# Smaller second load, one warm-up product for three, latents' transposes a chunk later in a one-core decoder layer

## The chip, the cores and the metric

One core of a Trainium2 chip runs the whole kernel. The metric is device time in microseconds. A row of a trace is stamped in microseconds from the start of the profiled span. TensorE is PE, VectorE is DVE, ScalarE is ACT, GpSimd is POOL, and SyncE (SP) issues the loads.

## The reference

For 256 tokens of width 1024 the layer computes, in float32:

```
proj = x @ W_in                      # c_q 256, c_kv 128, k_rope 32, then q, k, v of group B, 512 each
A = latent attention: rms_norm(c_q) @ w_uq, rms_norm(c_kv) @ w_ukv, rotary keys, 8 heads, causal
B = block attention over q, k, v of 8 heads; 256 keys are one block, so it is causal with ALiBi
x = LayerNorm(2**0.25 * x + concat(A, B) @ w_o)
x = LayerNorm(2**0.25 * x + FFN(x))  # FFN: up to 2*2816, causal conv of width 3, silu(g)*u, down
```

## The kernel before, in words

Every float32 operand of a large product is split in two rounded halves: `split` (lines 81 to 89) lets ACT cast the loaded tile to its high part `h_...` (L87) and DVE subtract to get the low part `l_...` (L88). A product is then three matmuls: high by high, high by low, low by high.

The stage that matters here is the first one. The input, transposed, comes in eight slices of 128 rows (`xraw`, 128 KB each), and so does the part of W_in that makes the latents (`w_c`: 128 rows by 416 columns, 208 KB a slice). `C_CHUNKS` says how many slices one load takes, as pairs (first slice, number); for each chunk SP issues the load of `xraw`, then that of `r_wc`, and each slice is cast and subtracted on its own. PE then accumulates `pc` for both halves of the tokens: six matmuls of 416 columns for a slice (L181 to L183). Before any data is there, `keep_warm` (L97 to L101) has PE multiply a zeroed tile: six products of 128 by 128, then three with 64 columns; in float32 each product is two matmul instructions.

Next come the values of group B, `pv` (L247): eight slices of w_v, six matmuls of 512 columns each. Inside this stage the normalised latents `cn` (they share the tile `ccn` with their transposed copy `cT`) are turned by PE, six 128 by 128 transposes into `pct` (L233); DVE scales each pair of them out of PSUM (L235), and ACT and DVE split the result into `chl` (L236, L237). `TURN_AFTER` is the slice of `pv` after which this is put. The queue projections `pq`, keys `pk` and the first `pqk` follow; then the heads' scores `sca`.

On PE the products of `pv`, the warm-up products and the transposes are pinned to the order in which they are written; from the first scores on, all matmuls are. What is not pinned is put in order by the framework's scheduler, which works from estimated costs: so a move of the transposes also moves instructions on DVE and ACT and the not yet pinned `pk`, `pq` and `pqk` products. Each engine then works its own list in order, and waits where an operand is not ready.

Of the kernel before, what the change touches and what calls it, by code (L numbers as in the profile page):

```python
# [14 lines left out]
P = 128  # L15
# [13 lines left out]
NEG = -1.0e30  # L29
CH = 1024  # L30

C_CHUNKS = ((0, 1), (1, 2), (3, 2), (5, 2), (7, 1))
V_CHUNKS = ((0, 2), (2, 2), (4, 2), (6, 2))
TURN_AFTER = 4
LAG = 2
BEFORE = 2
A0, A4 = 2, 0
WARM = (6, 5)
WARM_NARROW = 3
HELD = 6  # L40
HALVES = ((0, 512), (512, 512))
COLS = ((HALVES, HALVES), (HALVES, ((0, 512), (512, 256), (768, 256))))
# [9 lines left out]
def layer_kernel(ctx: ExitStack, tc: tile.TileContext, a, out):  # L52
    nc = tc.nc
# [11 lines left out]
    def wk_tile(name):  # L65
        return ps_wk.tile([P, HALF], F32, tag="wk", name=name)
# [27 lines left out]
    zero = const.tile([P, P], F32, name="zero")  # L94
    nc.vector.memset(zero, 0.0)

    def keep_warm(n, name, cols=P):  # L97

        warm = wk_tile(name)
        for _ in range(n):  # L100
            tc.keep_in_program_order(nc.tensor.matmul(warm[:, :cols], zero, zero[:, :cols], start=True, stop=True))  # L101

    keep_warm(WARM[0], "warm0")
    keep_warm(WARM_NARROW, "warm0n", P // 2)

    tabs = const.tile([P, 4], F32, name="tabs")

# [18 lines left out]
    wc = {}  # L126
    for k0, n in C_CHUNKS:
        ks = slice(k0, k0 + n)
# [98 lines left out]
    def turn_latents():  # L227
        for b0 in range(0, NB, 2):
            pt = wk_tile(f"pct{b0}")
            for b in range(b0, min(b0 + 2, NB)):  # L230
                for t in range(NT):
                    o = (b - b0) * S + t * P
                    tc.keep_in_program_order(nc.tensor.transpose(pt[:, o:o + P], cn[:, t, b * P:(b + 1) * P], ident))  # L233
                g = qg[:, b:b + 1] if b < 2 else kvg
                nc.vector.tensor_scalar(cT[:, b, :], pt[:, (b - b0) * S:(b - b0 + 1) * S], g, None, op0=ALU.mult)  # L235
        nc.scalar.copy(chi, cT)  # L236
        nc.vector.tensor_sub(clo, cT, chi.bitcast(F32))  # L237

    pv = [acc_tile(f"pv{t}") for t in range(NT)]
    for k0, n in V_CHUNKS:  # L240
        hi, lo = load_split(a["w_v"][:, k0 * HALF:(k0 + n) * HALF], n * HALF, f"wv{k0}", parts=n)
        for k in range(k0, k0 + n):
            o = (k - k0) * HALF
            for t in range(NT):
                tk = slice(t * P, (t + 1) * P)
                for i, (st, mv) in enumerate(((xhi, hi), (xhi, lo), (xlo, hi))):
                    tc.keep_in_program_order(nc.tensor.matmul(pv[t], st[:, k, tk], mv[:, o:o + HALF],  # L247
                                                              start=(k == 0 and i == 0), stop=(k == KT - 1 and i == 2)))
            if k == TURN_AFTER:
                turn_latents()  # L250
# [311 lines left out]

    a0, a4 = Turned(0, 0, 4, wk_tile), Turned(0, 4, 4, wk_tile)
    keep_warm(WARM[1], "warm1")
    a0.affine(True, 0, A0)
    ln_root(0, 1)
# [228 lines left out]
```

## Time and profile before

| what | value |
|---|---|
| median of 3 runs | 310.29 us (309.94 to 311.3) |
| the profiled execution | 308.82 us, of which the traced span is 307.0 us |
| PE busy | 296.1 us, 96% of the span |
| DVE, ACT, POOL busy | 77%, 65%, 10% |
| the chain that ended last | PE 92%, DVE 3%, DMA 2%, ACT 1% |
| mean granted TensorE clock | 0.994 |

The busy shares say that PE is the engine to look at; the chain of waits says the same by another way, since it follows the last instruction back to what released it. What is left is to find the few places where PE waits or runs slowly. The rows further down are from those places.

### The profile page before, as it was taken

To read this page: it belongs to the slowest core of one execution; us is meant where nothing else is said; L and a number is where in the kernel's file an instruction comes from. 1 tells how busy PE (TensorE), PEld (TensorE's weight loads), DVE (VectorE), ACT (ScalarE), POOL (GpSimd) and SP (SyncE) were. 2 spreads that over 40 slices of the span, in tenths; PEclk is the share of its full clock that TensorE was granted. 3 is DMA by queue.
4 is the path that set the end of the run, shared out by engine and by line. 5 is a ranking of instruction groups with operands and counts; after the bars stand their busy time and mean duration, and the time that the engine had idled before them with its cause. 6 is when DMAs were issued, how large, how long until landed. Compare 5 with 4: busy or idle time off the path is not lost.

```text
span 307.0 us, 4884 instructions
## 1 busy us (share of the span) xinstructions
PE 296.1 (96%) x1736; PEld 262.2 (85%) x1736; DVE 237.3 (77%) x475; ACT 198.8 (65%) x390; POOL 31.4 (10%) x43
## 2 busy tenths in 40 slices
PE   8999999999999989999999999999999999999990
PEld 7987999999888869888888888888888888888880
DVE  2878976656565387999999888888886978975595
ACT  4789996676655287977666657666676758634410
POOL 9430300035310021000000000000000000000030
PEclk9999999999999999999999999999999999999997
DMA  6998855273332104988865556555555776000003
GB/s 198 400 405 298 292 190 175 100 244 117 118 108 101 68 0 125 360 315 269 276 226 181 181 194 203 185 176 181 183 175 203 240 244 202 0 0 2 0 1 138
DMA packets 16216, 54.31 MB, mean 177 GB/s; under 512 B 1824, under 2 KB 2736, under 8 KB 16192
## 3 DMA queue, kind: packets, MB, share of 16 engines
q1 hardware_dynamic: 15840, 52.92, 49.7%
q0 software_dynamic: 352, 1.09, 1.2%
q8 instruction: 13, 0.21, 0.3%
q14 instruction: 11, 0.09, 0.1%
HBM read 52.95 MB, written 1.05 MB: 176 GB/s over the span
## 4 chain that ended last, share of the span: by engine, by line
PE 92%; DVE 3%; DMA 2%; ACT 1%; SPq 0%; issue 0%; DVEq 0%
PE ph L621 25%; PE pd L658 19%; PE ph L624 13%; PE pqk L279 7%; PE pm L279 7%; PE pv L247 4%; PE po L279 3%; PE pq L279 2%; PE sca L279 2%; DMA r_wc<-in_w_c 2%; PE scb L279 2%; PE pc L181 1%; PE ph L611 1%; PE ph L612 1%; PE ph L615 1%; PE pc L182 1%
## 5 line engine op out<-in xcount | busy, mean ns | idle before, releaser
L621 PE MATMUL ph<-x,h_wu 128*128 128x512 f32 x328 | 82.8, 393 | 0.0
L621 PEld LDWEIGHTS ph<-x,h_wu 128*128 128x128 f32 x328 | 59.1, 188 | 10.9
L88 DVE TENSOR_TENSOR l_wu<-r_wu,h_wu 128x1024 fp32r<-128x1024 f32 x44 | 53.5, 1219 | 7.7 <-ACT h_wu L87 7.3
L87 ACT CAST h_wu<-r_wu 128x1024 fp32r<-128x1024 f32 x44 | 45.8, 1048 | 6.2 <-PE ph L621 3.3
L633 DVE SCALAR_TENSOR_TENSOR hc<-h,cw,hc 128x255 f32<-128x255 f32 x82 | 39.3, 479 | 12.6 <-ACT hc L631 11.7
L624 PEld LDWEIGHTS ph<-x,l_wu 128*128 128x128 f32 x328 | 44.7, 190 | 3.4
L624 PE MATMUL ph<-x,l_wu 128*128 128x256 f32 x328 | 45.7, 282 | 0.0
L631 ACT ACTIVATE hc<-h,cw 128x256 f32<-128x256 f32 x41 | 24.6, 601 | 24.1 <-DVE h L628 24.1
L279 PE MATMUL pqk<-x,h_wqk 128*128 128x256 f32 x128 | 27.2, 298 | 0.0
L279 PEld LDWEIGHTS pqk<-x,h_wqk 128*128 128x128 f32 x128 | 20.6, 190 | 0.3
L88 DVE TENSOR_TENSOR l_wd<-r_wd,h_wd 128x1024 fp32r<-128x1024 f32 x16 | 19.5, 1220 | 0.9 <-ACT h_wd L87 0.9
L658 PE MATMUL pd<-l_wd,ghi 128*128 128x512 f32 (+1 forms) x80 | 20.1, 349 | 0.0
L658 PE MATMUL pd<-h_wd,glo 128*128 128x512 f32 (+1 forms) x80 | 20.1, 349 | 0.0
L658 PE MATMUL pd<-h_wd,ghi 128*128 128x512 f32 (+1 forms) x80 | 20.0, 348 | 0.0
L722 POOL TENSOR_TENSOR r<-r,lnv 128x512 f32<-128x512 f32 x1 | 1.3, 1293 | 180.8 <-ACT r L721 180.8
L279 PE MATMUL pqk<-x,l_wqk 128*128 128x256 f32 x64 | 19.1, 299 | 0.0
L628 DVE TENSOR_TENSOR h<-ph,hb 128x256 f32<-128x256 f32 x41 | 17.1, 417 | 2.0 <-ACT hb L626 2.0
L87 ACT CAST h_wd<-r_wd 128x1024 fp32r<-128x1024 f32 x16 | 16.7, 1045 | 2.8 <-PE ph L621 2.6
L645 ACT CAST ghi<-gt 128x256 fp32r<-128x256 f32 x22 | 8.9, 403 | 11.6 <-DVE gt L642 11.6
L658 PEld LDWEIGHTS pd<-h_wd,glo 128*128 128x128 f32 x80 | 14.0, 189 | 2.1
L658 PEld LDWEIGHTS pd<-l_wd,ghi 128*128 128x128 f32 x80 | 14.0, 189 | 2.1
L658 PEld LDWEIGHTS pd<-h_wd,ghi 128*128 128x128 f32 x80 | 14.0, 189 | 1.9
(166 smaller groups left out, 583.6 us busy)
## 6 DMA issues: line engine op xcount, KB each, us to landing
r_wu<-in_w_up SPq DMA_DIRECT2D x44, 512.0 KB, 3.7
r_wd<-in_w_down SPq DMA_DIRECT2D x22, 512.0 KB, 4.2
r_wqk<-in_w_qk SPq DMA_DIRECT2D x8, 512.0 KB, 5.1
r_wo<-in_w_o SPq DMA_DIRECT2D x8, 512.0 KB, 3.9
r_wv<-in_w_v SPq DMA_DIRECT2D x4, 512.0 KB, 7.7
lnv<-in_ln SPq DMA_DIRECT2D x4, 512.0 KB, 5.8
r_wc<-in_w_c SPq DMA_DIRECT2D x3, 416.0 KB, 6.6
r_wuq<-in_w_uq SPq DMA_DIRECT2D x2, 512.0 KB, 7.8
```

The costliest lines, as they stand in the source:

```text
L87: nc.scalar.copy(hi[:, c], raw[:, c])
L88: nc.vector.tensor_sub(lo[:, c], raw[:, c], hi[:, c].bitcast(F32))
L181: nc.tensor.matmul(pc[t][:, :NC0], xhi[:, k, tk], hi[:, o:o + NC0], start=(k == 0), stop=False)
L247: tc.keep_in_program_order(nc.tensor.matmul(pv[t], st[:, k, tk], mv[:, o:o + HALF], start=(k == 0 and i == 0), stop=(k == KT - 1 and i == 2)))
L279: ins = nc.tensor.matmul(*args, **kw)
L621: nc.tensor.matmul(ph, hi[:, ks], x1[:, k].rearrange("p i t -> p (i t)"), start=(k == 0), stop=False)
L624: nc.tensor.matmul(ph[:, :S], lo[:, ks], x1hi[:, k, :], start=False, stop=(k == KT - 1))
L628: nc.vector.tensor_tensor(h, ph[:, :S], hb, op=ALU.add)
L631: nc.scalar.activation(hc, h, AF.Identity, bias=c[:, 3:4], scale=c[:, 2:3])
L633: nc.vector.scalar_tensor_tensor(hc[:, j:S], h[:, 0:S - j], c[:, 2 - j:3 - j], hc[:, j:S], op0=ALU.mult, op1=ALU.add)
L645: rounded = nc.scalar.copy(ghi, gt)
L658: ins = nc.tensor.matmul(pd[t, o][:, :n], st[:, tk], mv[:, o:o + n], start=(f == 0 and i == 0), stop=(f == NF - 1 and i == 2))
```

## The change

Three numbers are changed. The first two slices are loaded one by one and the other six in pairs, where it was one, three pairs, and one. The warm-up is seven products of 128 columns and none of 64. The latents' transposes stand after slice 5 of `pv`, not after slice 4.

```diff
-C_CHUNKS = ((0, 1), (1, 2), (3, 2), (5, 2), (7, 1))
+C_CHUNKS = ((0, 1), (1, 1), (2, 2), (4, 2), (6, 2))
-TURN_AFTER = 4
+TURN_AFTER = 5
-WARM = (6, 5)
-WARM_NARROW = 3
+WARM = (7, 5)
...
-    def keep_warm(n, name, cols=P):
+    def keep_warm(n, name):
...
-            tc.keep_in_program_order(nc.tensor.matmul(warm[:, :cols], zero, zero[:, :cols], start=True, stop=True))
+            tc.keep_in_program_order(nc.tensor.matmul(warm[:, :P], zero, zero, start=True, stop=True))
 
     keep_warm(WARM[0], "warm0")
-    keep_warm(WARM_NARROW, "warm0n", P // 2)
```

Line numbers of the changed kernel are one or two lower than those used here. The numbers behind the tiles' names tell buffers apart; they differ between the two kernels where the tile is the same.

On ACT, at the start, the casts stood like this (the first `r_wc` is slice 0):

```order
L87 CAST x_101<-xraw 128x256
L87 CAST h_wc_105<-r_wc_103 128x416
L87 CAST x_101<-xraw 128x256 x2
L87 CAST h_wc_114<-r_wc_112 128x416 x2
L87 CAST x_101<-xraw 128x256 x2
```

and now stand like this:

```order
L86 CAST x_98<-xraw 128x256
L86 CAST h_wc_102<-r_wc_100 128x416
L86 CAST x_98<-xraw 128x256
L86 CAST h_wc_111<-r_wc_109 128x416
L86 CAST x_98<-xraw 128x256 x2
L86 CAST h_wc_120<-r_wc_118 128x416 x2
```

Slice 1 is now cast when it has come alone, and slices 2 and 3 come together. DVE's subtractions are moved in the same way.

On DVE, from the last scaling of the latents by their root to the first `qT`, in before (`l_wqk_436` is the low part of the first group-B weights, `chl` the low part of the turned latents):

```order
L235 TENSOR_SCALAR ccn_240<-pct0_333,vecs_181 128x256
L88 TENSOR_TENSOR l_wuq0_381<-r_wuq0_378,h_wuq0_380 128x1024
L235 TENSOR_SCALAR ccn_240<-pct0_333,vecs_181 128x256
L235 TENSOR_SCALAR ccn_240<-pct2_340,vecs_181 128x256
L88 TENSOR_TENSOR l_wuq1_387<-r_wuq1_384,h_wuq1_386 128x1024
L88 TENSOR_TENSOR l_wukv_393<-r_wukv_390,h_wukv_392 128x1024
L237 TENSOR_TENSOR chl_276<-ccn_240,chl_276 128x768
L88 TENSOR_TENSOR l_wqk00_436<-r_wqk00_433,h_wqk00_435 128x1024
L88 TENSOR_TENSOR l_wqk10_576<-r_wqk10_573,h_wqk10_575 128x1024
L312 TENSOR_TENSOR qT_376<-pq0_419,qtab_186 128x512
```

and now:

```order
L87 TENSOR_TENSOR l_wuq0_378<-r_wuq0_375,h_wuq0_377 128x1024
L233 TENSOR_SCALAR ccn_237<-pct0_336,vecs_178 128x256
L87 TENSOR_TENSOR l_wuq1_384<-r_wuq1_381,h_wuq1_383 128x1024
L233 TENSOR_SCALAR ccn_237<-pct0_336,vecs_178 128x256
L233 TENSOR_SCALAR ccn_237<-pct2_343,vecs_178 128x256
L87 TENSOR_TENSOR l_wukv_390<-r_wukv_387,h_wukv_389 128x1024
L87 TENSOR_TENSOR l_wqk00_433<-r_wqk00_430,h_wqk00_432 128x1024
L235 TENSOR_TENSOR chl_273<-ccn_237,chl_273 128x768
L87 TENSOR_TENSOR l_wqk10_573<-r_wqk10_570,h_wqk10_572 128x1024
L87 TENSOR_TENSOR l_wqk01_632<-r_wqk01_629,h_wqk01_631 128x1024
L310 TENSOR_TENSOR qT_373<-pq0_416,qtab_183 128x512
```

A weight subtraction now stands ahead of the first scaling, and another ahead of `chl`'s low part and of `qT`.

On PE, behind `pv` and the transposes of the rotary keys, ten products of the first `pqk` have moved ahead of those of `pk` and `pq` that need the low part of `chl`; it now reads:

```order
L277 MATMUL pq_416<-chl,h_wuq_377 128x256
L277 MATMUL pq_416<-chl,l_wuq_378 128x256
L277 MATMUL pqk_436<-x_98,h_wqk_432 128x256 x2
L277 MATMUL pqk_436<-x_98,l_wqk_433 128x256
L277 MATMUL pqk_436<-x_98,h_wqk_432 128x256 x2
L277 MATMUL pqk_436<-x_98,l_wqk_433 128x256
L277 MATMUL pqk_436<-x_98,h_wqk_432 128x256 x2
L277 MATMUL pqk_436<-x_98,l_wqk_433 128x256
L277 MATMUL pqk_436<-x_98,h_wqk_432 128x256
L277 MATMUL pk_407<-chl,h_wukv 128x256 x2
```

In before, `pk` and `pq` went on after the second of these rows, and all 24 products of `pqk` came behind them.

## Rows read from the trace of the kernel before

**Rows 1.** Page, chain that ended last: shares of the span by engine.

```profile
PE 92%; DVE 3%; DMA 2%; ACT 1%; SPq 0%; issue 0%; DVEq 0%
```

**Rows 2.** Timeline, PE, 0 to 17 us: start, us, engine, line, out<-in, count, [idle before].

```profile
1.05 2.93 PE L101 MATMUL warm<-zero 128*128 128x128 f32 x12 [1.05 <-DVE zero L95]
...
3.77 1.38 PE L101 MATMUL warm0n<-zero 128*128 128x64 f32 x6
...
5.47 1.06 PE L181 MATMUL pc<-h_wc,x 128*128 128x416 f32 x2 [0.32 <-ACT h_wc L87]
...
6.33 0.55 PE L182 MATMUL pc<-l_wc,x 128*128 128x416 f32 x1
...
7.37 0.55 PE L183 MATMUL pc<-h_wc,x 128*128 128x416 f32 x1
...
7.96 1.06 PE L181 MATMUL pc<-h_wc,x 128*128 128x416 f32 x2
...
8.82 0.55 PE L182 MATMUL pc<-l_wc,x 128*128 128x416 f32 x1
...
9.52 0.36 PE L182 MATMUL pc<-l_wc,x 128*128 128x416 f32 x1
...
16.48 0.35 PE L183 MATMUL pc<-h_wc,x 128*128 128x416 f32 x1
```

**Rows 3.** Windows: stretch, length, busy us of each engine, granted clock, DMA share, GB/s.

```profile
5.40:9.40 4.00, 3.88 (x10) 3.02 (x11) 2.78 (x6) 2.42 (x7) 3.80 (x4) 1.00 0.96 350
```

**Rows 4.** Timeline, ACT and DVE, the splits of slices 0 to 4.

```profile
4.88 0.54 ACT L87 CAST h_wc<-r_wc 128x416 fp32r<-128x416 f32 x1 [1.18 <-DMA r_wc<-in_w_c]
...
5.57 0.71 ACT L87 CAST x<-xraw 128x256 fp32r<-128x256 f32 x2 [0.15 <-DMA xraw<-in_xT]
...
7.37 0.98 ACT L87 CAST h_wc<-r_wc 128x416 fp32r<-128x416 f32 x2 [1.08 <-DMA r_wc<-in_w_c]
7.94 1.40 DVE L88 TENSOR_TENSOR l_wc<-r_wc,h_wc 128x416 fp32r<-128x416 f32 x2 [1.17 <-ACT h_wc L87]
...
9.69 0.98 ACT L87 CAST h_wc<-r_wc 128x416 fp32r<-128x416 f32 x2 [0.55 <-DMA r_wc<-in_w_c]
```

**Rows 5.** Timeline, PE, DVE and ACT, around the transposes.

```profile
23.11 1.98 ACT L87 CAST h_wuq<-r_wuq 128x1024 fp32r<-128x1024 f32 x2
...
23.51 0.38 PE L233 MATMUL pct<-ident,ccn 128*128 128x128 f32 x2
23.93 0.48 DVE L235 TENSOR_SCALAR ccn<-pct,vecs 128x256 f32<-128x256 f32 x1 [0.97 <-PE pct L233]
24.34 1.21 DVE L88 TENSOR_TENSOR l_wuq<-r_wuq,h_wuq 128x1024 fp32r<-128x1024 f32 x1
...
24.47 0.66 PE L233 MATMUL pct<-ident,ccn 128*128 128x128 f32 x4 [0.58 <-DVE ccn L235]
...
25.47 0.87 DVE L235 TENSOR_SCALAR ccn<-pct,vecs 128x256 f32<-128x256 f32 x2
```

**Rows 6.** Chain in order of time: start, us, what; `pv` behind the transposes.

```profile
25.13 4.10 PE pv L247 x18
```

**Rows 7.** Timeline, ACT, DVE and PE, from the turned latents to the first scores.

```profile
26.25 1.21 DVE L88 TENSOR_TENSOR l_wuq<-r_wuq,h_wuq 128x1024 fp32r<-128x1024 f32 x1
...
27.39 1.22 DVE L88 TENSOR_TENSOR l_wukv<-r_wukv,h_wukv 128x1024 fp32r<-128x1024 f32 x1
...
28.52 0.95 DVE L237 TENSOR_TENSOR chl<-ccn,chl 128x768 fp32r<-128x768 f32 x1
28.59 0.59 ACT L252 COPY v_b<-pv 128x512 f32<-128x512 f32 x1 [0.43 <-PE pv L247]
...
29.21 0.37 PE L279 MATMUL pk<-chl,h_wukv 128*128 128x256 f32 x1
...
29.39 2.35 DVE L88 TENSOR_TENSOR l_wqk<-r_wqk,h_wqk 128x1024 fp32r<-128x1024 f32 x2
...
31.66 0.68 DVE L312 TENSOR_TENSOR qT<-pq,qtab 128x512 f32<-128x512 f32 x1
...
34.29 0.82 PE L279 MATMUL sca<-kT,qT 128*128 128x128 f32 x4
```

## The prediction, made before the changed kernel ran

> **What bounds the kernel now.** I read the chain of waits first: 92% of it is PE [rows 1], so a change counts by what it does to PE's list, and whatever PE loses or wins in the first 35 us is carried to the end, unless a later wait takes it up. Then the timeline of PE in the stretch that the change touches. The reader is to see three things there. PE's 416-column products start 0.347 us apart at first (6.33 to 7.37 in three steps) and 0.188 us apart later (9.52 to 16.48 in 37 steps) [rows 2]: 416 columns at the two clock levels, 1.2 and 2.4 GHz, take 0.347 and 0.173. So the clock rose at about 9.45, though the column of the granted clock reads 1.00 in the slow stretch [rows 3]; I go by the spacing. Second, while slow, PE waits twice on slice 1: the product due at 7.72 (7.37 + 0.347) starts at 7.96, and the one due at 8.65 (7.96 + 2 x 0.347) starts at 8.82 [rows 2]. From there to the transposes it has no gap: the spacing holds over all 37 steps. Third, at the transposes PE does two at 23.51 and the other four only at 24.47, when DVE's first scaling is written [rows 5].
>
> **The change part by part.**
>
> Loads. Before and after there are two single chunks and three pairs, so the transfers are the same and only their order is new. Slice 1's weights came with slice 2's in 416 KB, and the cast that had waited for them started at 7.37 [rows 4]. By bytes: 336 KB had landed when the first weight cast started (4.88), 592 at 5.57, 1008 at 7.37, 1680 at 9.69 [rows 4]. After the change slice 1 is complete at 672 KB, on that line at 5.9. Its cast (0.54) then ends near 6.5 and its subtraction (at most 0.70, half of 1.40) near 7.2, before PE wants them at 7.72 and 8.41. Both waits go: 0.24 + 0.17 = 0.41 us at half clock, which is 1.2 products, worth 1.2 x 0.188 = 0.22 us if the clock rises when it did. The bounds: nothing gained if slice 1 lands as late as the pair did, and 0.41 if the clock is up already. Next late could be slices 2 and 3, complete at 1344 KB, on the line at 8.5 (bounds 7.4 and 9.7); cast ends 9.1 and 9.6, subtractions about 9.7 and 10.4. PE, now 0.22 ahead, takes slice 2's first high product at 9.6, its low one at 10.0, and slice 3 at 10.8: just covered. At the late bound PE would wait some 0.6, which turns the 0.22 into a loss of 0.4. Slices 4 and 5 (2016 KB, about 10.6) and 6 and 7 (12.4) are wanted at 11.9 and 14.1, with more than half a microsecond of cover after their split.
>
> Warm-up. Six products of 128 columns took from 1.05 to 3.77 with their weight loads, 0.45 each; the three narrow ones 1.38 together, 0.46 each [rows 2]: half the columns, no less time. Seven wide ones end near 4.2 where the old row ended at 5.15. Nothing waits for them; the first real product waits for the cast that ends at 5.42 [rows 2, 4], so the direct cost is 0. PE's idle time before it grows from 0.32 to about 1.2. What that does to the clock no row of before shows, so it is bounded: at no effect the rise stays at 9.45 and the cost is 0; a rise later by d costs d x (1 - 0.188 / 0.347) = 0.46 d. I take 0, since the rise came only after 4 us of real products, 4.3 us past the warm-up's end at 5.15, and that stretch becomes denser, not thinner.
>
> The Trainium skill, on the page "TensorE: Matmul & The Clock Gate" (section "HAM oscillation — how this bites in real kernels"), speaks against this edit: waiting gaps of PE put the clock back to the slow level, so each burst behind one starts slow. By it a warm-up that stops early has been wasted; by the rows above it had not raised the clock in any case. It is weighed as the slow rival below.
>
> Transposes. Six `pv` products stand now ahead of them: 6 x 4.10 / 18 = 1.37 [rows 6], so (on the clock of before) the first two transposes start at 24.88. DVE has `l_wuq0` ahead of the first scaling; its high part is cast by 23.11 + 0.99 = 24.10 [rows 5], so it starts at 24.16. Going by start to start on DVE (1.14 for a weight from 26.25 to 27.39, 0.41 for one scaling from 23.93 to 24.34, 0.78 for two from 25.47 to 26.25 [rows 5, 7]) the first scaling starts at 25.30. PE went on 0.54 after that start (23.93 to 24.47 [rows 5]), so now at 25.84, which is 0.96 after its first transpose, exactly as before: 0.00. The wait is moved, not removed. If the ACT side does not come 0.22 earlier along with PE, the 0.22 is lost here.
>
> Behind them. The second weight starts at 25.71, the two scalings at 26.85, `l_wukv` at 27.63, `l_wqk00` at 28.77, ending at 29.99 (1.22). PE's first `pk` product stays at 29.21, and its steps are (34.29 - 29.21) / 42 = 0.121 (4 + 14 + 24 products [rows 7]). The first low `pqk` product is the seventh, due at 29.21 + 6 x 0.121 = 29.94, and can start at 30.05: a new wait of 0.11. The ten pulled-ahead products then end at 31.0; `chl`'s low part is written at 29.91 + 0.95 = 30.86, in time: without the ten, PE would have waited for it since 29.7. `qT` now stands behind `l_wqk10` and `l_wqk01`. Their casts queue behind two `v_b` copies and a smaller one on ACT, from 28.59 on (0.59 each [rows 7], the smaller taken the same at most): casts done by 31.3 and 32.3, subtractions started at 31.35 and 32.5, `qT` from 33.6 to 34.3 (0.68). The scores want it at 34.29 + 0.11 = 34.40. That is covered by 0.1, and whatever these casts are later beyond that is a wait.
>
> Sum: -0.22 + 0 + 0.00 + 0.11 = -0.11 us. The profiled execution took 308.82 us, its span 307.0 and 1.8 around it; it becomes 308.7. It stands 1.47 below the median of the runs, so on their scale 310.29 - 0.11 = 310.2 us.
>
> **The rivals.**
>
> Slow: the clock. If the rise in before, 8.4 us after PE's first product, was prepared by the warm-up across a gap of only 0.32, and the longer gap makes that count start at 5.47 instead of 1.05, the rise comes 4.4 us later: 4.4 x 0.46 = 2.0 us. With the rest 312.2. For it: the narrow products fill the time to the first data nearly to the end. Against it: PE was busy from 1.05 to 5.15 and the clock did not rise in that. It decides where the wide spacing is still seen beyond 11.5 (below, it is worth under 1 us).
>
> Slow, smaller: a queue on DVE. If `l_wuq0`, `l_wqk00` or the pair before `qT` is late by one weight subtraction (1.2 us), PE waits for as much at the transposes or before the scores: 311.3. For it: three waits with cover of 0.1 or less. Against it: the casts they need are shifted with PE.
>
> Fast: with slices 0 and 1 unbroken the clock rises sooner. Were it up at 5.47, the data would bind: slice 2 from 9.1, with its low part at 9.7, its end at 10.5, five more slices of 6 x 0.188 = 1.13, end at 16.1, against 16.44 (16.66 - 0.22). Another 0.3: 309.9.
>
> No gain at all: slice 1 or slices 2 and 3 land late, 310.3 to 310.8.
>
> **How the numbers follow.** Forecast 0.48, no gain 0.14, fast clock 0.12, DVE queue 0.13, slow clock 0.13. The forecast's own range is 309.7 to 310.8. A measurement of this kernel can tell about 0.5%, 1.55 us, from no change: all cases but the slow clock lie within. The runs themselves spread from 309.94 to 311.3, and medians may differ by chance; I give that 0.08 to the fast side and put slower at 0.13. The range reaches from 309.1, a spread's worth below the fast rival, to 312.0, which leaves out most of the slow clock.
>
> **What would show it.** Right: the second group of six `pc` products follows the first with no gap; wide spacing until about 9.5; one idle stretch before the last four transposes, of 0.5 to 0.7; a short wait before the third `pqk` product. Wrong: wide spacing beyond 11.5 (clock); a wait of PE on a cast of slices 2 or 3; over 1 us idle at the transposes, or PE waiting for `qT`.

## The result, and the profile after

The changed kernel takes 311.71 us, the median of 14 runs (310.52 to 315.73), against 310.27 for 14 runs of the kernel before on the same chip. The ratio is 1.0056 with a 95% interval of [1.0036, 1.0077]: slower, by 1.1 to 2.4 us. The ratio compares fast executions alone and is not the quotient of the two medians. The forecast was 310.2, no change to be measured, with a chance of 0.13 for slower. The time lies inside the range (309.1 to 312.0); the direction was missed.

The profiled execution of the changed kernel took 312.34 us, its span 310.6, against 308.82 and 307.0. That is 3.5 us and more than twice the difference of the medians, because each profile is one execution: the one of before stands 1.45 below its median, the one of after 0.63 above. What the two traces show therefore has to be weighed before it is called the change's. Start times of the same work in both:

| us | before | after | later by |
|---|---|---|---|
| first `pc` product | 5.47 | 5.27 | -0.20 |
| first `pv` product (end of the compression) | 16.67 | 17.54 | 0.87 |
| first `pk` product | 29.21 | 30.08 | 0.87 |
| first scores | 34.29 | 36.42 | 2.13 |
| first product of the feed-forward part | 114.18 | 116.36 | 2.18 |
| end of the last down product | 299.27 | 302.79 | 3.52 |

So there are three losses: 0.87 before `pv`, another 1.26 between `pk` and the scores, and 1.34 near the end. Between `pv` and `pk`, where the transposes moved, nothing changes.

**At the scores.** The timeline of after, PE, ACT, DVE and POOL, against [rows 7], with the two copies and the two subtractions as single instructions (from windows that hold one of each):

```profile
30.08 0.37 PE L277 MATMUL pk<-chl,h_wukv 128*128 128x256 f32 x1
30.76 0.95 DVE L235 TENSOR_TENSOR chl<-ccn,chl 128x768 fp32r<-128x768 f32 x1
30.89 2.01 ACT L86 CAST h_wqk<-r_wqk 128x1024 fp32r<-128x1024 f32 x2
30.90 0.39 PE L277 MATMUL pqk<-x,l_wqk 128*128 128x256 f32 x1
31.13 1.50 POOL L272 COPY kT<-ksb 64x1024 f32<-64x1024 f32 x1 [9.63 <-ACT ksb L270]
31.99 1.71 DVE L87 TENSOR_TENSOR l_wqk<-r_wqk,h_wqk 128x1024 fp32r<-128x1024 f32 x1 [0.28 <-ACT h_wqk L86]
32.68 1.92 POOL L272 COPY kT<-ksb 64x1024 f32<-64x1024 f32 x1
33.62 2.06 DVE L87 TENSOR_TENSOR l_wqk<-r_wqk,h_wqk 128x1024 fp32r<-128x1024 f32 x1
35.16 0.28 PE L277 MATMUL pqk<-x,l_wqk 128*128 128x256 f32 x1
35.37 1.04 ACT L86 CAST h_wqk<-r_wqk 128x1024 fp32r<-128x1024 f32 x1 [0.31 <-PE pqk L277]
35.60 0.68 DVE L310 TENSOR_TENSOR qT<-pq,qtab 128x512 f32<-128x512 f32 x1
36.42 0.89 PE L277 MATMUL sca<-kT,qT 128*128 128x128 f32 x4 [0.98 <-ACT h_wqk L86]
```

PE stands idle for 0.98 us before the scores, where before it had no gap. The row names ACT's `h_wqk` as what ended the wait, since a cast ended just then (35.37 + 1.04 = 36.41). But the scores don't need that cast: in E5, E6, E7 and E9 below they start before it has ended (in E9 at 34.66, with the cast from 34.68 to 35.73). The last input to arrive was `qT`, written at 35.60 + 0.68 = 36.28. And `qT` was late because the two weight subtractions ahead of it on DVE took 35.60 - 31.99 = 3.61 us from start to start. In before, two of them took 31.66 - 29.39 = 2.27 [rows 7].

The single rows say where the 1.34 us between these went. Both subtractions start while one of POOL's copies into `kT` runs, and DVE and POOL finish in turn: `chl` at 31.71, the first copy at 32.63, the first subtraction at 33.70, the second copy at 34.60, the second subtraction at 35.68. Each end comes 0.90 to 1.08 us after the one before it, about what one such instruction takes by itself (a subtraction 1.14 from start to start [rows 7], two copies 2.15 in E10, where no subtraction ran beside them). So they ran one at a time, as far as the rows show: the first subtraction lasted 0.49 longer than the 1.22 it takes alone, the second 0.85 longer than 1.21, and 0.49 + 0.85 = 1.34.

Of the 1.26 us from `pk` to the scores, 1.14 is this wait (the scores were due at 35.16 + 0.12 = 35.28). The other 0.12 is a short wait for `l_wqk00`, the first low part of group B: the product at 30.90 fills 0.39 where its like fill 0.28.

The trace of before held the warning, in rows that the prediction did not use:

```profile
31.00 2.75 POOL L274 COPY kT<-ksb 64x1024 f32<-64x1024 f32 x2 [10.36 <-ACT ksb L272]
...
33.07 2.90 DVE L88 TENSOR_TENSOR l_wqk<-r_wqk,h_wqk 128x1024 fp32r<-128x1024 f32 x2 [0.73 <-ACT h_wqk L87]
```

There, too, a pair that starts beside the end of the copies took 2.90 us instead of 2.35, behind `qT`, where nobody waited for it.

**At the start.** PE's timeline of after, against [rows 2]:

```profile
5.27 1.06 PE L179 MATMUL pc<-h_wc,x 128*128 128x416 f32 x2 [0.86 <-ACT h_wc L86]
...
7.17 0.55 PE L181 MATMUL pc<-h_wc,x 128*128 128x416 f32 x1
7.51 0.90 PE L179 MATMUL pc<-h_wc,x 128*128 128x416 f32 x2
...
9.25 0.55 PE L181 MATMUL pc<-h_wc,x 128*128 128x416 f32 x1
10.39 0.64 PE L179 MATMUL pc<-h_wc,x 128*128 128x416 f32 x2 [0.60 <-ACT h_wc L86]
11.02 0.45 PE L180 MATMUL pc<-l_wc,x 128*128 128x416 f32 x1
11.31 0.35 PE L181 MATMUL pc<-h_wc,x 128*128 128x416 f32 x1
```

Slice 1 follows slice 0 without a gap (7.17, 7.51), as forecast: both waits of 0.24 and 0.17 are gone. But slice 2 is late: PE waits 0.60 for its weights. And the spacing goes from 0.347 to 0.188 only near 11.1, not at 9.45. The whole 0.87 can be put together from this: the products that run before the spacing narrows are 15 instead of 10, at (11.31 - 5.27 - 0.60) / 15 = 0.363 each instead of 0.188, 0.88 us; the waits are 0.60 instead of 0.41; the first product is 0.20 earlier. 0.88 + 0.19 - 0.20 = 0.87. The casts on ACT, in the timeline of after, say when the data came [against rows 4]:

```profile
6.72 0.54 ACT L86 CAST h_wc<-r_wc 128x416 fp32r<-128x416 f32 x1 [1.20 <-DMA r_wc<-in_w_c]
...
8.71 0.71 ACT L86 CAST x<-xraw 128x256 fp32r<-128x256 f32 x2 [1.45 <-DMA xraw<-in_xT]
9.80 0.98 ACT L86 CAST h_wc<-r_wc 128x416 fp32r<-128x416 f32 x2 [0.39 <-DMA r_wc<-in_w_c]
```

Slice 1 came at 6.7 and not at 5.9, slices 2 and 3 at 9.8 and not at 8.5. The windows view of the first 9 us (length, busy us of PE, weight loads, DVE, ACT, POOL, granted clock, DMA share, GB/s), of before:

```profile
0.00:9.00 9.00, 7.59 (x27) 6.55 (x28) 2.97 (x7) 4.68 (x10) 8.15 (x21) 1.00 0.72 227
```

and of after:

```profile
0.00:9.00 9.00, 7.09 (x25) 6.37 (x26) 2.11 (x5) 3.57 (x7) 8.06 (x22) 1.00 0.69 196
```

196 GB/s for 227: by 9 us, some 280 KB less has moved. The same bytes in another order did not keep the line by bytes.

**At the transposes.** The timeline of after, PE and DVE, against [rows 5]:

```profile
25.04 1.23 DVE L87 TENSOR_TENSOR l_wuq<-r_wuq,h_wuq 128x1024 fp32r<-128x1024 f32 x1 [1.21 <-ACT h_wuq L86]
25.75 0.38 PE L231 MATMUL pct<-ident,ccn 128*128 128x128 f32 x2
26.18 0.48 DVE L233 TENSOR_SCALAR ccn<-pct,vecs 128x256 f32<-128x256 f32 x1
26.71 0.66 PE L231 MATMUL pct<-ident,ccn 128*128 128x128 f32 x4 [0.58 <-DVE ccn L233]
```

The same 0.96 from the first pair to the others, the same 0.58 idle. The wait was moved, not removed.

**Near the end.** PE's timeline of after:

```profile
294.11 0.73 PE L656 MATMUL pd<-hd,ghi 128*128 128x512 f32 x2 [1.07 <-ACT ghi L643]
```

This wait of 1.07 us stands in the profile of after and not in that of before. The experiments below show that it is not the change's.

### The profile page after: what moved, and what is told of

The parts are those of the page before. It is cut to its first block, busy times and chain, and to the rows that moved or that the text cites. A ratio compares the mean times of both kernels' runs of the same rounds, so it can differ in the third digit from the quotient of the medians.

```text
span 310.6 us, 4875 instructions
## 1 busy us (share of the span) xinstructions
PE 296.4 (95%) x1732; PEld 261.4 (84%) x1732; DVE 238.3 (77%) x475; ACT 198.9 (64%) x390; POOL 31.2 (10%) x43
## 4 chain that ended last, share of the span: by engine, by line
PE 70%; DVE 13%; DMA 8%; ACT 5%; issue 1%; SPq 1%; DVEq 0%; ACTq 0%
PE ph L619 16%; PE pd L656 12%; PE ph L622 8%; PE pqk L277 7%; PE pm L277 7%; DMA r_wd<-in_w_down 6%; PE pv L245 4%; PE po L277 3%; DVE hc L631 3%; DVE l_wu L87 2%; DMA r_wc<-in_w_c 2%; DVE ld L87 2%; PE pq L277 2%; PE sca L277 2%; PE scb L277 2%; ACT hd L86 1%
```

## The experiments

Each kernel was timed beside the kernel before, on the same chip; before's medians were 309.91 (E1 to E4), 310.19 (E5 to E8) and 310.44 (E9 to E12). All readings in one table. "Old" or "new" is the row of loads; `pv` is the start of the first of its products, `pk` to `sca` the time from the first `pk` product to the scores (before: 5.08), "tail" from the first feed-forward product to the last down product, GB/s the mean of the first 9 us. These columns are of one profiled execution of each kernel; the ratios are of 6 to 14 runs of it.

| kernel | loads | GB/s | `pv` | `pk` to `sca` | tail | ratio to before, 95% |
|---|---|---|---|---|---|---|
| before | old | 227 | 16.67 | 5.08 | 185.09 | 1 |
| after | new | 196 | 17.54 | 6.34 | 186.43 | 1.0056 [1.0036, 1.0077] |
| E1 turn only | old | 230 | 16.62 | 6.34 | 186.06 | 1.0047 [1.0021, 1.0072] |
| E2 loads and warm-up | new | 205 | 17.16 | 5.08 | 187.01 | 1.0024 [1.0001, 1.0046] |
| E3 loads only | new | 205 | 19.06 | 5.08 | 186.72 | 1.0016 [0.9998, 1.0034] |
| E4 warm-up only | old | 229 | 17.25 | 5.05 | 186.07 | 1.0019 [0.9998, 1.0040] |
| E5 after, `qT` first | new | 198 | 17.03 | 5.17 | 187.39 | 1.0010 [0.9980, 1.0041] |
| E6 turn only, `qT` first | old | 221 | 16.55 | 5.18 | 186.41 | 1.0003 [0.9983, 1.0022] |
| E7 `qT` late | old | 229 | 16.79 | 5.25 | 185.06 | 1.0013 [0.9987, 1.0039] |
| E8 own tiles | old | 225 | 16.33 | 5.15 | 186.16 | 0.9986 [0.9961, 1.0011] |
| E9 less on POOL | new | 199 | 16.86 | 5.21 | 185.54 | 1.0025 [1.0002, 1.0048] |
| E10 two queues | new | 244 | 17.12 | 5.07 | 187.21 | 1.0102 [1.0070, 1.0134] |
| E11 nine warm-up products | new | 202 | 16.87 | 5.16 | 187.71 | 1.0030 [1.0004, 1.0056] |
| E12 own tiles, two queues | old | 257 | 16.06 | 5.07 | 186.30 | 0.9983 [0.9962, 1.0004] |

### E1 to E4: the parts alone

**E1**, the kernel before with the later turn alone:

```diff
-TURN_AFTER = 4
+TURN_AFTER = 5
```

> The kernel before with the transposes one chunk later and nothing else. Theory Q (the loss is at the first scores: qT now stands on VectorE behind two weight subtractions, one of which runs beside GpSimd's copies and takes 2.05 us for 1.22): PE idle about 1.0 us before the first scores, time 0.8 to 1.2 us over the kernel before. Theory S (the loss is made in the first 12 us, by slices 2 and 3 landing late and the clock rising later): no idle there that counts, time within 0.3 us of before.

312.3 us for 309.91, ratio 1.0047 [1.0021, 1.0072]. The timeline of E1, PE and DVE, shows the wait of after again with the old start:

```profile
29.18 0.37 PE L279 MATMUL pk<-chl,h_wukv 128*128 128x256 f32 x1
31.08 3.69 DVE L88 TENSOR_TENSOR l_wqk<-r_wqk,h_wqk 128x1024 fp32r<-128x1024 f32 x2 [0.28 <-ACT h_wqk L87]
34.70 0.68 DVE L312 TENSOR_TENSOR qT<-pq,qtab 128x512 f32<-128x512 f32 x1
35.52 0.89 PE L279 MATMUL sca<-kT,qT 128*128 128x128 f32 x4 [1.00 <-ACT h_wqk L87]
```

`pv` and `pk` start within 0.05 of before's; the scores start 1.23 later. The later turn alone brings most of the slowdown: 0.7 to 2.2 us by the interval, with the 0.8 to 1.2 of theory Q in it.

**E2**, the changed kernel with the turn put back:

```diff
-TURN_AFTER = 5
+TURN_AFTER = 4
```

> The changed kernel with the transposes put back behind slice 4: new chunks and seven warm-up products only. Theory S: group-B values start 0.8 to 1.0 us later than in before, PE waits about 0.6 us for slice 2, wide spacing of the 416-column products until about 11; time 0.8 to 1.1 us over before. Theory Q: no idle before the first scores, time within 0.3 us of before.

310.97 us, ratio 1.0024 [1.0001, 1.0046]. The way from `pk` to the scores is 5.08 again, as theory Q says, and `pv` starts 0.49 late, about half of what theory S says; PE waits 0.34 for slice 2. The interval holds the times of both theories.

**E3**, the kernel before with the new loads alone:

```diff
-C_CHUNKS = ((0, 1), (1, 2), (3, 2), (5, 2), (7, 1))
+C_CHUNKS = ((0, 1), (1, 1), (2, 2), (4, 2), (6, 2))
```

> The kernel before with the new chunks only, the narrow warm-up products kept. If the late slices 2 and 3 are the cost: PE waits 0.5 to 0.8 us for slice 2 here too and the time is 0.5 to 1.0 us over before. If the shorter warm-up is the cost (by the clock): the clock rises by 9.5 as in before, and the time is within 0.3 us of before or below it by 0.2.

310.36 us, ratio 1.0016 [0.9998, 1.0034]. PE's timeline of E3:

```profile
8.07 0.34 PE L183 MATMUL pc<-h_wc,x 128*128 128x416 f32 x1
10.35 0.65 PE L181 MATMUL pc<-h_wc,x 128*128 128x416 f32 x2 [1.93 <-ACT h_wc L87]
...
11.49 0.55 PE L183 MATMUL pc<-h_wc,x 128*128 128x416 f32 x1
11.84 0.55 PE L182 MATMUL pc<-l_wc,x 128*128 128x416 f32 x1
```

In this execution the fast spacing came early, PE was through slice 1 at 8.3 and waited 1.93 us for slice 2. From 11.49 on the products are 0.35 apart again, until 14.3. Its profiled run was the slowest of its 13 (312.83), so the 19.06 of the table is an extreme; but it shows what a late slice can set off. The Trainium skill says the same on its page "TensorE: Matmul & The Clock Gate" (section "HAM oscillation — how this bites in real kernels"): gaps in which PE waits put the clock back to its slow level. This trace agrees, by the spacing, behind a gap of 1.93 us; behind the 0.60 of after the spacing narrowed within 0.7 us, and behind 1.10 in E8 and 1.19 in E11 it stayed narrow.

**E4**, the kernel before with the new warm-up alone:

```diff
-WARM = (6, 5)
-WARM_NARROW = 3
+WARM = (7, 5)
...
```

> The kernel before with seven wide warm-up products only, chunks and transposes as before. If the longer idle of PE ahead of the first data keeps the clock low: wide spacing until about 11 or beyond, time 0.5 to 1.0 us over before. If the late slices are the cost: wide spacing until about 9.5, time within 0.3 us of before.

310.71 us, ratio 1.0019 [0.9998, 1.0040]. The fast spacing came near 10.4, `pv` 0.58 late. Alone, this cannot be told from no effect.

### E5 to E7: is it the place of `qT`?

**E5**, the changed kernel with `qT` ahead of `l_wqk01` again. It differs from after by that one swap on DVE:

```diff
+    q_ins = {}
...
-        nc.vector.tensor_tensor(qT[...], ..., qtab, op=ALU.mult)
+        q_ins[pr] = nc.vector.tensor_tensor(qT[...], ..., qtab, op=ALU.mult)
...
-        hi, lo = load_split(a["w_qk"][w * 4 + pr], CH, f"wqk{w}{pr}")
+        with tc.issue_after(q_ins[0].ins) if pr else nullcontext():
+            hi, lo = load_split(a["w_qk"][w * 4 + pr], CH, f"wqk{w}{pr}")
```

> The changed kernel with one instruction put back: qT ahead of the low part of the third group-B weight on VectorE, where it stood before; all else in the changed order. Theory Q (qT's place is the cost of moving the transposes): no idle of PE before the first scores, which come 5.1 to 5.3 us after the first pk product instead of 6.34; time 0.2 to 0.8 us over before (what the chunks and the warm-up cost), 1.0 to 1.3 below the changed kernel. Rival R (the cost lies in the other reordering, ten pqk products ahead of pk and pq, or in chl's low part): the scores still come 6.0 us or more after the first pk product and the time stays 1.3 us or more over before.

310.1 us for 310.19, ratio 1.0010 [0.9980, 1.0041]. The timeline of E5, DVE and PE:

```profile
31.51 1.68 DVE L87 TENSOR_TENSOR l_wqk<-r_wqk,h_wqk 128x1024 fp32r<-128x1024 f32 x1 [0.30 <-ACT h_wqk L86]
33.31 0.69 DVE L312 TENSOR_TENSOR qT<-pq,qtab 128x512 f32<-128x512 f32 x1
33.92 2.40 DVE L87 TENSOR_TENSOR l_wqk<-r_wqk,h_wqk 128x1024 fp32r<-128x1024 f32 x2
34.78 0.82 PE L277 MATMUL sca<-kT,qT 128*128 128x128 f32 x4
```

One subtraction, still long (1.68) beside the copies, then `qT` at 33.31; no gap before the scores. The two behind it, clear of the copies for the most part, take 2.40 together. After's interval and this one still meet (1.0036 to 1.0041), so it is the trace, 5.17 from `pk` to the scores for 6.34, that tells theory Q from rival R. The 0.09 left over the 5.08 of before is the wait for `l_wqk00`; E6 has it too.

**E6**, the later turn alone with the same edit as in E5:

> The kernel before with the transposes one chunk later, and qT kept ahead of the low part of the third group-B weight. Theory Q: within 0.4 us of before. Rival R: 1.0 to 1.5 us over before, as with the transposes moved alone.

310.16 us, ratio 1.0003 [0.9983, 1.0022], where E1 had 1.0047 (the intervals touch at 1.0021 to 1.0022). With E1 and E5 this shows the main cause: the turn does its harm through `qT`'s place on DVE, and without that it costs nothing that can be measured.

**E7**, the kernel before, turn unchanged, with `qT` put behind `l_wqk01`:

```diff
...
+    for w, pr in ((0, 0), (1, 0), (0, 1)):
+        early[w, pr] = load_split(a["w_qk"][w * 4 + pr], CH, f"wqk{w}{pr}")
+    early_sub = split.last
...
-        nc.vector.tensor_tensor(qT[...], ..., qtab, op=ALU.mult)
+        with tc.issue_after(early_sub.ins) if pr == 0 else nullcontext():
+            nc.vector.tensor_tensor(qT[...], ..., qtab, op=ALU.mult)
...
```

> The kernel before, transposes, chunks and warm-up untouched, with qT put behind the low part of the third group-B weight on VectorE (and with it, on ScalarE, the first two kT copies behind that weight's cast). Theory Q: PE idle 0.9 to 1.2 us before the first scores, time 0.9 to 1.4 us over before, as with the transposes moved. Rival R: within 0.4 us of before.

310.83 us, ratio 1.0013 [0.9987, 1.0039], and the scores only 0.17 later than in before, counted from `pk`: theory Q, which had `qT`'s place alone cost 0.9 to 1.4 us, missed here. The timeline of E7, DVE and POOL:

```profile
28.59 0.95 DVE L237 TENSOR_TENSOR chl<-ccn,chl 128x768 fp32r<-128x768 f32 x1
29.46 4.34 DVE L88 TENSOR_TENSOR l_wqk<-r_wqk,h_wqk 128x1024 fp32r<-128x1024 f32 x3
31.09 3.61 POOL L279 COPY kT<-ksb 64x1024 f32<-64x1024 f32 x2 [10.35 <-ACT ksb L277]
33.72 0.68 DVE L318 TENSOR_TENSOR qT<-pq,qtab 128x512 f32<-128x512 f32 x1
```

With the early turn DVE is done with `chl` at 29.5 (in after at 31.7) and starts its weights before the copies: three of them take 4.26, of which only the last lies beside a copy, and `qT` still comes nearly in time. So the place of `qT` alone is not enough; it needs the later turn as well, which pushes the subtractions into the copies.

### E8 and E12: the wait at the transposes

**E8**, the kernel before, each pair of transposes in a PSUM tile of its own:

```diff
-        for b0 in range(0, NB, 2):
+        for b0 in range(NB):
...
-            for b in range(b0, min(b0 + 2, NB)):
+            for b in range(b0, b0 + 1):
```

> The kernel before with each pair of the latents' transposes in a PSUM tile of its own instead of two pairs in one. If the wait at the transposes comes from the shared tile (the second pair written while VectorE still reads the first): PE's 0.58 us idle there goes to 0.2 or less and the time is 0.3 to 0.6 us below before, unless the scheduler's other order behind it gives that back. If it comes from the latents themselves or the copy's tile: the idle stays near 0.58 and the time within 0.3 us.

310.01 us, ratio 0.9986 [0.9961, 1.0011]. PE's timeline of E8:

```profile
23.19 0.82 PE L233 MATMUL pct<-ident,ccn 128*128 128x128 f32 x6
```

All six run in one piece; the 0.58 idle is gone, and `pv` to `pk` falls from 12.54 to 11.75. So it was the shared tile, not the turn's place, that made this wait. Whether the whole kernel gains by it the interval leaves open.

**E12**, E8 with the input's loads issued by ACT, so that SP has half the issues of the start:

```diff
+    for k0, n in C_CHUNKS:
+        nc.scalar.dma_start(xraw[:, k0:k0 + n, :], a["xT"][:, k0:k0 + n, :])
...
-        nc.sync.dma_start(xraw[:, ks, :], a["xT"][:, ks, :])
```

> The kernel before with both helps together: each pair of the transposes in a PSUM tile of its own, and the loads of xraw issued by ScalarE. If the idle at the transposes (0.6 us) and the issue of the first loads both cost time: 0.7 to 1.4 us below before. If the start is bound by the memory or by the casts: 0.2 to 0.6 us below before, as with the tiles alone.

310.08 us for 310.44, ratio 0.9983 [0.9962, 1.0004]. The first 9 us move 257 GB/s and `pv` starts at 16.06, the earliest of all, but the order that the scheduler makes puts 0.96 us of waiting back at the transposes, here for the last of the normalised latents. The interval, from 1.2 below before to 0.1 over it, leaves both forecasts open. The best of the study, and not clearly better than before.

### E9: is it POOL's copies?

**E9**, the changed kernel with POOL copying only the first of each four pairs of heads. The rest of the rotary part of `kT` is left zero, so the scores of the other pairs lack it:

```diff
...
+    with tc.issue_after(kr_done.ins):
+        nc.gpsimd.memset(kT, 0.0)
...
-            nc.gpsimd.tensor_copy(kT[rows, j], ksb[rows].to_broadcast([NOPE, H // 2, S]))
+            nc.gpsimd.tensor_copy(kT[rows, j, 0:1], ksb[rows])
```

> The changed kernel, order unchanged, with GpSimd's two copies of the rotary keys cut to the first of their four pairs (kT is zeroed before, so the scores of the other pairs are left without their rotary part). Theory P (qT is late because the two weight subtractions ahead of it run beside these copies): the two subtractions take 2.3 to 2.6 us from start to start instead of 3.61, PE's idle before the first scores falls from 0.98 to 0.2 or less, time 0.8 to 1.2 us below the changed kernel, so 0.2 to 0.7 over before. Theory O (qT's place alone makes it late, whatever runs beside): idle 0.7 or more, time as the changed kernel, about 1.5 over before.

311.1 us for 310.44, ratio 1.0025 [1.0002, 1.0048]: the rest that E2 also shows. The timeline of E9, POOL and DVE:

```profile
30.50 2.33 POOL L275 COPY kT<-ksb 64x256 f32<-64x256 f32 x2 [7.90 <-ACT ksb L273]
31.35 2.56 DVE L87 TENSOR_TENSOR l_wqk<-r_wqk,h_wqk 128x1024 fp32r<-128x1024 f32 x2 [0.30 <-ACT h_wqk L86]
33.84 0.68 DVE L313 TENSOR_TENSOR qT<-pq,qtab 128x512 f32<-128x512 f32 x1
```

`qT` is still behind both subtractions, but these take 2.49 from start to start instead of 3.61, and PE has no gap before the scores (5.21 from `pk`). That is what theory P said. By the time alone, 0.1 to 1.5 us over before, theory O's 1.5 would stand at the edge. The stretch on DVE is the copies' doing.

The plainest view of it is in E8, where the first copy starts beside two subtractions that follow each other without a gap. DVE and POOL in the timeline of E8:

```profile
29.06 2.35 DVE L88 TENSOR_TENSOR l_wqk<-r_wqk,h_wqk 128x1024 fp32r<-128x1024 f32 x2
29.12 3.20 POOL L274 COPY kT<-ksb 64x1024 f32<-64x1024 f32 x1 [8.83 <-ACT ksb L272]
```

Here the subtractions lose nothing, and the copy, begun at 29.12, ends at 32.32, 0.91 after both. So it is not always DVE that waits. The Trainium skill, on the page "SBUF — State Buffer" (section "Who interferes with whom"), has the rule for it: a DVE instruction with two inputs in SBUF contends with a GpSimd instruction that reads SBUF, over ports that are held as an exclusive lock. The subtraction has two such inputs and the copy reads one, and the traces agree, in after by the ends in turn and in E8 by the copy that outlasts both subtractions.

### E10 and E11: the start

**E10**, E5's kernel with the input's loads issued by ACT, as in E12:

> The kernel of the fifth experiment (the changed one with qT ahead) with the five loads of xraw issued by ScalarE instead of SyncE, so that two engines issue at once. Theory I (slices 2 and 3 land late because SyncE issues one load each 0.47 us and small loads first keep few bytes in flight): 2000 KB or more moved in the first 9 us instead of 1760 to 1850, slice 2's weights landed by 9.2 at the latest instead of 9.75, group-B values started by 16.8, time 0.3 to 0.8 us below the fifth experiment's. Theory B (the bytes land at the rate that the memory gives, whoever issues): the same bytes within 60 KB and group-B values at 17.0 or later.

313.14 us, ratio 1.0102 [1.0070, 1.0134], from six runs. The windows row of E10 for the first 9 us, and after it, from its timeline, PE at the transposes:

```profile
0.00:9.00 9.00, 6.42 (x23) 5.91 (x24) 2.50 (x6) 3.91 (x8) 8.07 (x22) 1.00 0.77 244
```

```profile
27.58 0.66 PE L232 MATMUL pct<-ident,ccn 128*128 128x128 f32 x4 [1.87 <-DVE ccn L234]
```

244 GB/s for 198 in E5: the rate at the start does hang on how the loads are issued. But ACT casts later while it issues (the first product starts at 5.93), and the scheduler's new order opens 1.87 us at the transposes. `pv` starts at 17.12, not by 16.8 as theory I had it. As a test of the time the run is spoilt by all this.

**E11**, E5's kernel with a longer warm-up:

```diff
-WARM = (7, 5)
+WARM = (9, 5)
```

> The kernel of the fifth experiment with nine warm-up products instead of seven, which end about 0.9 us later, near the first data. If the idle time of PE ahead of the first data holds the clock down: wide spacing ends by 8 or earlier, and the time is 0.3 to 0.8 us below the fifth experiment's. If the clock's rise doesn't hang on that: the time is within 0.3 us of it.

310.85 us, ratio 1.0030 [1.0004, 1.0056]. PE's timeline of E11:

```profile
6.26 0.36 PE L179 MATMUL pc<-h_wc,x 128*128 128x416 f32 x1
6.45 0.35 PE L180 MATMUL pc<-l_wc,x 128*128 128x416 f32 x1
...
8.20 0.34 PE L181 MATMUL pc<-h_wc,x 128*128 128x416 f32 x1
9.74 0.65 PE L179 MATMUL pc<-h_wc,x 128*128 128x416 f32 x2 [1.19 <-ACT h_wc L86]
```

Fast spacing from 6.2, and then 1.19 us of waiting for slice 2. E5, with seven warm-up products, had the narrow spacing by 5.9 too, so this run doesn't show that the longer warm-up brought it. With the new loads an early clock buys nothing: the data bind. Where it came early with the old loads (E8, near 6.0) `pv` started at 16.33, with the new ones (E5, E11, near 6) at 17.03 and 16.87.

### The wait near the end

The tail is 185.09 in before's profile and 185.06 in E7's; in the other twelve it is 185.5 to 187.7, each with PE waiting 0.16 to 2.33 us before the last down products. That includes E8 and E12, which have the old loads and the old turn and whose ratios are below one. So this wait doesn't hang on the change. That other executions of before have it too is inferred: its one profile is of an execution without it, 1.45 below the median. What the wait hangs on stays open. The chain of waits by engine looks quite different with it: in E8, which has this wait and neither of the two other losses, PE's share is 71%, in E7, which lacks it, 92% as in [rows 1]. That is the main reason why after's chain reads:

```profile
PE 70%; DVE 13%; DMA 8%; ACT 5%; issue 1%; SPq 1%; DVEq 0%; ACTq 0%
```

## Why the prediction was wrong

**The step that failed** is the last one behind the transposes: "subtractions started at 31.35 and 32.5, `qT` from 33.6 to 34.3 (0.68). The scores want it at 34.29 + 0.11 = 34.40. That is covered by 0.1". The order was right, the casts came in time, the place was right; the duration of the two subtractions was not. On after's clock (0.87 later) the chain forecast 32.22 for the first subtraction and 34.47 for `qT`. The first started at 31.99, even earlier, and `qT` at 35.60: 3.61 us for two instead of the 2.27 of [rows 7], because each stood behind one of POOL's copies. The 2.27 came from a pair that a copy met only at its end, at 31.00, and there it was the copies that lost time (2.75 for the 2.15 of E10). Cover of 0.1 became a wait of 0.98, and with it nearly all of the 1.26 us between `pk` and the scores. E1 alone gives 1.0047, E6 takes it back, E9 removes the cause and the wait.

**The rival "a queue on DVE"** had this place and nearly this price (one weight subtraction, 1.2; 311.3 in all) with a chance of 0.13. What the prediction held against it, that the casts are shifted with PE, was true and beside the point: nothing arrived late, the work itself took longer.

**The start**, -0.22, came out the other way. Right: slice 1's waits are gone. Wrong: the landing of slices 2 and 3 by bytes at 8.5. In after's profile the late bound, 9.7, is what came true (9.80), and with it the wait of 0.6 that the prediction had worked out for that case. The load of these weights took 6.7 us from issue to landing, that of the old pair (slices 3 and 4) in the same place of the row of issues 6.6, though fewer bytes lay ahead of it. But 9.80 is the latest of the six profiles with the new loads from one queue, in which ACT begins on slice 2's weights at 8.66 to 9.80: always behind the line by bytes, and mostly ahead of the old third load (9.38 to 9.76). One reading was off as well: the 0.17 was no wait for slice 1's low part. The two products behind a stall fill 1.06 (7.96 and 5.47 in before, 5.27 in after), the two at 7.51 in after, behind none, 0.90; so it went with the stall of 0.24.

E2, E3, E5, E9 and E11, all with the new loads and without the wait for `qT`, have ratios from 1.0010 to 1.0030; so the new start, loads and warm-up together, is worth about 0.2%, some 0.6 us, with most of the single intervals reaching close to one. How that divides between loads (E3, 1.0016) and warm-up (E4, 1.0019) the runs don't tell.

**The warm-up**, 0: no row shows a price of its own (E4, 1.0019 [0.9998, 1.0040]). The clock rival had the fast spacing come 4.4 us later; after's came 1.65 later, below the 11.5 at which the prediction let it count. But over the fourteen profiles the spacing narrowed anywhere from 5.5 to 11.1, and kernels that share start and warm-up differ (E2 7.5, E5 5.9, E9 10.3). So the 0.88 that it costs in after's profile belongs in part to this one execution. Sorted by warm-up, the profiles point the clock rival's way, on a smaller scale: with the old one the spacing narrowed at 9.0 to 9.5 in four of seven, with seven wide products at 10.3 to 11.1 in four of six, and in all others by 7.5. With one execution of each kernel that is a hint and not shown; what the shorter warm-up itself does stays open.

**The fast rival** (clock up at once, `pv` at 16.1) fell: E5 and E11 had the clock and met late data.

**The transposes** came out exactly: 0.96 between the pairs, 0.00 gained. The wait of 0.11 for `l_wqk00` came out as well: 0.12 in after, 0.09 and 0.10 left in E5 and E6.

**The sum.** The later turn's 0.47% and about 0.2% of the start make some 0.7%, where the change measures 0.56% [0.36, 0.77]. In the profiled pair the same three parts read 1.26, 0.87 and 1.34, of which the last is not the change's and the middle one not all of it.

## What to carry to other kernels

When an instruction is moved, take its duration from a row in which it runs beside what it will run beside; a subtraction that takes 1.2 us alone and 1.7 to 2.1 behind another engine's copy was in the trace of before (the pair of 2.90), in the one place where nobody waited for it. A cover of 0.1 us in a chain of five steps is no cover: it should carry a price and a chance like a wait. And when loads are put in another order, don't trust a line through the bytes alone: take the landing of the load in the same place of the old row as the late bound, give it a chance, and ask which load is late next.

## What the runs showed of the hardware

- A 128x1024 subtraction on DVE takes 1.21 us by itself and up to 2.06 in after beside GpSimd's 64x1024 copies; two in a row took 3.61 for 2.27. The two engines finish in turn, 0.90 to 1.08 us apart; in E8 it is the copy that waits, 3.20 us for one.
- With one issuing queue, a second small load ahead of the larger ones lowers the mean rate of the first 9 us from 221-230 to 196-205 GB/s in every profile; issuing half of the loads from a second engine raises it to 244 (E10) and 257 (E12).
- The time at which PE's spacing narrows from 0.347 to 0.188 us varies from 5.5 to 11.1 us over the fourteen profiles, and from 5.9 to 11.1 between after, E2, E5 and E9, whose loads and warm-up are the same; the column of the granted clock reads 1.00 on both sides of it.
